# Four token-row chunks of an encoder's MLP moved from its start to its end, with VectorE block transposes in place of identity products

## The chip, the core and the metric

The kernel runs on one core of a Trainium2 chip. Its time is the device time of one execution in microseconds (us). A core has a matrix engine (TensorE, PE in the profile; its weight loads are listed apart as PEld), VectorE (DVE), ScalarE (ACT), GpSimd (POOL) and SyncE (SP), which here issues nearly all transfers. Matrix products write to PSUM; everything else lies in SBUF, with 128 partitions.

## The reference

Two layers of an encoder over 256 tokens of width 1024, each of a token mixer (pooling, dilated attention, gates) and a gated MLP, with RMSNorm ahead of each and a residual addition behind it. The change touches the MLP:

```python
def _conv_ffn(xn, w_up, conv_w, conv_b, w_down):
    a, gval = jnp.split(xn @ w_up, 2, axis=-1)
    a = lax.conv_general_dilated(a, conv_w[:, None, :], window_strides=(1,),
                                 padding=((CONV_WIDTH // 2, CONV_WIDTH // 2),),
                                 dimension_numbers=('NWC', 'WIO', 'NWC'),
                                 feature_group_count=D_FF) + conv_b
    return (jax.nn.gelu(a) * gval) @ w_down
```

`a` and `gval` are 256 x 2816 each. The convolution has width 3 and runs over the tokens, channel by channel.

## The kernel before, in words

**Layout.** Activations are kept with channels on the partitions, 128 at a time, and the tokens of even and odd number apart: `t` is 0 or 1, and token 2m + t stands at place m of half t. The 2816 MLP channels are NF = 22 chunks of 128. Each value is split into a high part in the matrix engine's fp32r type and the rest as a low part, and a product of two such values is taken as three products: high by high, high by low, low by high.

**Weights.** `Weights` (L81 on) streams all weights through the core in one order, which the calls of `W.use` write down (L235 to L282). A load brings 1 MB by one transfer on SyncE's queue (L117) into one of three raw buffers; it holds two pieces of 128 x 1024 elements. `open_next` turns a piece into its high part on ScalarE (L177) and its low part on VectorE (L178), in one of five buffers or, where a slot is named, in the buffer of a big tile that is idle then. `get` hands out the next piece and splits up to three more ahead (four more if they have a slot). A new load waits until the splits have read the raw buffer that it takes.

**A chunk by projection.** `proj` (L495 on, its products in `two_sums`, L487 to L493) takes one weight piece as the stationary operand and x2, the normed activations in high and low part, as the moving one: eight products of 512 columns (L491) and eight of 256 (L493). The result has channels on the partitions. `add_up` sums its two halves with one ScalarE copy (L513) and one VectorE addition (L514). The PSUM pool `mmp` has four buffers, and each projection takes one.

**The MLP's entry.** Of the first ENTRY = 4 chunks, `a` comes from another form: the products with x2 as the stationary operand and 512 columns of w_up as the moving one (`v_sum`, L583 on, L588; 24 products for each t). Their result has tokens on the partitions ("token rows"). For t = 0 this starts while the residual addition of the token mixer still runs (`begin_mlp`): x2's half t = 0 is complete earlier than t = 1. ScalarE copies the rows to SBUF (`keep_entry`, L1062), and `turn_entry` turns them to channels by four products with the identity matrix (L1068) and a VectorE copy from PSUM (L1070), once for each t. The group for t = 0 stands in the middle of the row products of t = 1; that for t = 1 stands behind the first projection, of chunk 0's `g`.

**The loop.** `up(f)` computes chunk f: it takes `a` (by projection from chunk 4 on), its `g` by projection, the convolution (L1094, L1095, L1098), the gelu in its tanh form (L1107 to L1112), the product with `g` (L1115), and the split of the result into high and low part (L1120, L1121). The loop takes two chunks at a time. From f = LAG = 6 on it adds two steps of `down` (`residual_mm`, L518 to L520), each with twelve products of 512 columns, for chunks f - 6 and f - 5. Behind the loop the last six steps follow; of the last four, the products are held back and taken output by output, so that the norm of the next sub-layer can begin early.

**Order.** PE, VectorE and ScalarE run their instructions in an order which a scheduler makes from the program's order and a cost model; a ready instruction can be drawn ahead of others. Each engine then runs its list in that order.

Of the kernel before, what the change touches and what calls it, by code (L numbers as in the profile page):

```python
# [10 lines left out]
F32 = mybir.dt.float32  # L11
# [5 lines left out]
P = 128  # L17
D = 1024
S = 256
# [8 lines left out]
NF = DFF // P  # L28
# [9 lines left out]
PAIRS = (2, 4, 0, 1, 3, 5)  # L38
LAG = 6
ENTRY = 4  # L40
HALVES = (slice(0, 512), slice(512, D))
SEGMENTS = (HALVES, (slice(0, 512), slice(512, 768), slice(768, D)))

# [161 lines left out]
def encoder(ctx, tc, x, w_in, w_pool, pool_scale, w_a, w_b, w_o, norm1, norm2, w_up, conv_w,  # L205
            conv_b, w_down, rel_bias, norm_f, onehot, edges, out):
    nc = tc.nc
    const = ctx.enter_context(tc.tile_pool(name="const", bufs=1))
    wpool = ctx.enter_context(tc.tile_pool(name="weights", bufs=1))
    big = ctx.enter_context(tc.tile_pool(name="big", bufs=1))  # L210
    sm = ctx.enter_context(tc.tile_pool(name="small", bufs=2))
    acc = ctx.enter_context(tc.tile_pool(name="acc", bufs=4, space=bass.MemoryType.PSUM))
    mmp = ctx.enter_context(tc.tile_pool(name="mmp", bufs=4, space=bass.MemoryType.PSUM))
# [3 lines left out]
    W = Weights(tc, wpool, big)  # L217

    def cols(w, c0):

        src = w[:, c0 : c0 + 256].rearrange("(k p) c -> p k c", p=P)
        return W.add(
            src, (8, 256), [((lambda t, j=j: t[:, :, j * P : (j + 1) * P]), (8, P)) for j in (0, 1)]
        )

    def rows(w, r0, n=2, c0=0, width=1024, tag=None, pieces=2):

        src = w[r0 : r0 + n * P, c0 : c0 + width].rearrange("(k p) c -> p k c", p=P)
        h = n // pieces
        return W.add(  # L230
            src, (n, width), [((lambda t, j=j: t[:, j * h : (j + 1) * h, :]), (h, width)) for j in range(pieces)],
            tag,
        )

    for l in range(DEPTH):  # L235
        for g in range(NG):
            c0 = C_V + g * 512
            slots = (("m2", 0, 2), ("m2", 1, 2), ("ybig",), ("at2",)) if g == 0 else ()
            for j in range(2):
                tag = "k1" if l == 0 and g == 1 and j == 0 else None  # L240
                W.use(rows(w_in[l], j * 512, 4, c0, 512, tag), slots[2 * j : 2 * j + 2])
        if l == 0:
            W.n_scaled = len(W.pieces)
        for c in range(3, -1, -1):
            W.use(cols(w_in[l], c * 256))
        for n, c in enumerate(PAIRS):
            pool = ([], [])
            if n == 1:
                pool = W.add(
                    w_pool[l].rearrange("g (k p) c -> p (g k) c", p=P), (8, 256),  # L250
                    [((lambda t, j=j: t[:, 4 * j : 4 * j + 4, :]), (4, 256)) for j in range(2)],
                )
                pool = (pool[:1], pool[1:])
            W.use(pool[0] + cols(w_in[l], C_Q + c * 256))
            W.use(pool[1] + cols(w_in[l], C_K + c * 256))
        for c in range(4):
            W.use(cols(w_a[l], c * 256))
        for c in range(4):
            W.use(cols(w_in[l], C_GP + c * 256))
        for c in range(2):  # L260
            W.use(cols(w_in[l], C_GA + c * 512))
            W.use(cols(w_in[l], C_GA + c * 512 + 256))
            src = w_b[l][:, c * 512 : (c + 1) * 512].rearrange("(k p) c -> p k c", p=P)
            W.use(
                W.add(
                    src, (4, 512),
                    [((lambda t, j=j: t[:, :, j * 256 : (j + 1) * 256]), (4, 256)) for j in (0, 1)],
                )
            )
        for c in range(4):  # L270
            W.use(rows(w_o[l], c * 256))
        slots = (("v1",), ("ybig",), ("at2",))
        for j in range(2):
            W.use(rows(w_up[l], j * 512, 4, 0, 512), slots[2 * j : 2 * j + 2])
        for f in range(0, NF, 2):
            a = cols(w_up[l], f * P) if f >= ENTRY else []
            g = cols(w_up[l], DFF + f * P)
            W.use([a[0], g[0], a[1], g[1]] if a else g)
            if f >= LAG:
                W.use(rows(w_down[l], (f - LAG) * P))  # L280
        for f in range(NF - LAG, NF, 2):
            W.use(rows(w_down[l], f * P))  # L282
# [10 lines left out]
    ident = const.tile([P, P], F32, name="ident")  # L293
# [201 lines left out]
    def proj(x2):  # L495

        i, (wh, wl) = W.get()
        ps = mmp.tile([P, 2, S], F32, tag="mm", name="proj_ps")
        two_sums(ps, lambda k: wh[:, k, :], lambda k: wl[:, k, :], x2, KD)
        W.free(i)  # L500
        return ps[:, 0], ps[:, 1]
# [78 lines left out]
    def v_tile():  # L580
        return acc.tile([P, 512], F32, tag="acc", name="v_ps")

    def v_sum(ps, x2, t, n, piece):  # L583

        _, (wh, wl) = piece
        passes = [(0, wh, 0), (0, wl, 0), (1, wh, 0), (0, wh, 1), (0, wl, 1), (1, wh, 1)]
        for m, (part, w, j) in enumerate(passes):
            nc.tensor.matmul(  # L588
                ps, x2[:, 2 * n + j, part, t, :], w[:, j, :], start=(n + m == 0),
                stop=(n == 3 and m == 5),  # L590
            )

    def two_parts(tag, name):

# [163 lines left out]
    for l in range(DEPTH):  # L758
# [21 lines left out]
        if l == 0:  # L780
            with tc.manual_schedule():
                begun = begin_values_of_x()
            x2 = first_values(*begun, keep_values)
        else:
            for g in range(NG):
                held = begun[0] if g == 0 else [W.get() for _ in range(4)]
                for t in range(2):
                    if g + t == 0:
                        ps = begun[1]
                    else:  # L790
                        ps = v_tile()
# [16 lines left out]
        for gi in range(3, -1, -1):  # L808
# [8 lines left out]
            cur, n = u, S + 2 * PAD  # L817
# [13 lines left out]
            if hw > 1:  # L831
                e = edge[:, gi, hw : w - 1].unsqueeze(1).to_broadcast([P, 2, hw - 1])
                r = slice(o + S - hw + 1, o + S)
# [109 lines left out]
        for pair in ((0, 1), (2, 3)):  # L943
            a, b = pair
# [110 lines left out]
        acts = {}  # L1055


        a_first = big.tile([P, ENTRY, S], F32, tag="gates", name="a_first")

        def keep_entry(ps):  # L1060
            r = sm.tile([P, ENTRY * P], F32, tag="p", bufs=3, name="a_rows")
            nc.scalar.copy(out=r, in_=ps)  # L1062
            return r

        def turn_entry(t, r):
            pt = mmp.tile([P, ENTRY, P], F32, tag="mm", name="a_turn")
            for f in range(ENTRY):
                nc.tensor.transpose(pt[:, f, :], r[:, f * P : (f + 1) * P], ident)  # L1068
            av = a_first.rearrange("p f (m t) -> p f m t", t=2)[:, :, :, t]
            nc.vector.tensor_copy(av, pt)  # L1070

        held, ps = entry
        first = keep_entry(ps)
        ps = v_tile()
        for n in range(4):
            v_sum(ps, x2, 1, n, held[n])
            if n == 1:
                turn_entry(0, first)
        for i, _ in held:
            W.free(i)  # L1080
        last = keep_entry(ps)
        g_first = [proj(x2)]
        turn_entry(1, last)

        def up(f):
            w0, w1, w2, b = (prm[:, l, j * NF + f : j * NF + f + 1] for j in range(4))
            if f < ENTRY:
                a = a_first[:, f, :]
            else:
                a = sm.tile([P, S], F32, tag="u", name="a")  # L1090
                add_up(in_order(a), [halves(b) for b in proj(x2)])
            sums = g_first.pop() if f == 0 else proj(x2)
            y = sm.tile([P, S], F32, tag="s", name="y")
            nc.scalar.activation(y, a, AF.Identity, bias=b, scale=w1)  # L1094
            nc.vector.scalar_tensor_tensor(  # L1095
                out=y[:, 1:], in0=a[:, : S - 1], scalar=w0, in1=y[:, 1:], op0=ALU.mult, op1=ALU.add
            )
            nc.vector.scalar_tensor_tensor(  # L1098
                out=y[:, : S - 1], in0=a[:, 1:], scalar=w2, in1=y[:, : S - 1],
                op0=ALU.mult, op1=ALU.add,  # L1100
            )
            g = sm.tile([P, 2, P], F32, tag="p", bufs=3, name="g")
            add_up(g, [halves(a) for a in sums])

            c = float(np.sqrt(2.0 / np.pi))
            y2 = sm.tile([P, S], F32, tag="us", name="y2")
            nc.scalar.activation(y2, y, AF.Square, scale=float(np.sqrt(0.044715)))  # L1107
            nc.vector.scalar_tensor_tensor(  # L1108
                out=y2, in0=y2, scalar=1.0, in1=y, op0=ALU.add, op1=ALU.mult
            )  # L1110
            nc.scalar.activation(y2, y2, AF.Tanh, scale=c)  # L1111
            nc.vector.scalar_tensor_tensor(  # L1112
                out=y2, in0=y2, scalar=1.0, in1=y, op0=ALU.add, op1=ALU.mult
            )
            nc.vector.scalar_tensor_tensor(  # L1115
                out=g, in0=in_order(y2), scalar=0.5, in1=g, op0=ALU.mult, op1=ALU.mult
            )
            n = f % NH
            ah, al = (x[n >= HPG][:, n - HPG * (n >= HPG)] for x in (acth, actl))
            nc.scalar.copy(out=ah, in_=g)  # L1120
            nc.vector.tensor_sub(out=al, in0=g, in1=ah.bitcast(F32))  # L1121
            acts[f] = (ah, al)
# [58 lines left out]
```

## Time and profile before

| | |
|---|---|
| median of three runs | 881.05 us (880.59 to 881.76) |
| the profiled execution | 880.87 us |
| its span, first to last instruction | 879.1 us |
| mean granted TensorE clock | 0.998 of full speed |
| bytes read from HBM | 162.74 MB |

The profile is of one execution. Rows with one line of the kernel, one engine and one operation are groups: busy time, mean ns of one, and what ended the idle time before them. The chain is the sequence of work that ended last, followed back from the last instruction. In the chain and the timeline the first column is the start in us from the span's start, the second the length in us. A view of waits lists the waiting engine and line, the releaser, us in total, number of times, and the longest one. In a view of stretches each engine's busy us stand with the number of its instructions, then the granted clock, the busy share of the transfer engines, and GB/s.

### The profile page before, as it was taken

To read this page: it belongs to the slowest core of one execution; us is meant where nothing else is said; L and a number is where in the kernel's file an instruction comes from. 1 tells how busy PE (TensorE), PEld (TensorE's weight loads), DVE (VectorE), ACT (ScalarE), POOL (GpSimd) and SP (SyncE) were. 2 spreads that over 40 slices of the span, in tenths; PEclk is the share of its full clock that TensorE was granted. 3 is DMA by queue.
4 is the path that set the end of the run, shared out by engine and by line. 5 is a ranking of instruction groups with operands and counts; after the bars stand their busy time and mean duration, and the time that the engine had idled before them with its cause. 6 is when DMAs were issued, how large, how long until landed. Compare 5 with 4: busy or idle time off the path is not lost.

```text
span 879.1 us, 12834 instructions
## 1 busy us (share of the span) xinstructions
PE 871.3 (99%) x4842; PEld 759.4 (86%) x4842; DVE 677.3 (77%) x1150; ACT 520.3 (59%) x913; POOL 14.7 (2%) x45
## 2 busy tenths in 40 slices
PE   9999999999999999999999999999999999999997
PEld 7888899988888888888888898999888888888886
DVE  6998786767869987787756977776678698878774
ACT  6755554556648766666545565554566486656653
POOL 2000000000000000000000000000000000000000
PEclk9999999999999999999999999999999999999999
DMA  9669744355554665565736565443556447466541
GB/s 325 237 232 304 229 145 157 131 190 183 172 198 149 212 215 192 168 215 192 240 120 227 157 200 184 154 158 124 191 189 199 164 147 255 170 195 204 178 144 48
DMA packets 126090, 164.64 MB, mean 187 GB/s; under 512 B 3254, under 2 KB 106374, under 8 KB 125900
## 3 DMA queue, kind: packets, MB, share of 16 engines
q1 hardware_dynamic: 126012, 163.82, 56.2%
q8 instruction: 38, 0.62, 0.3%
q14 instruction: 24, 0.20, 0.1%
q10 hardware_dynamic: 16, 0.00, 0.0%
HBM read 162.74 MB, written 3.69 MB: 189 GB/s over the span
## 4 chain that ended last, share of the span: by engine, by line
PE 96%; DVE 2%; DMA 1%; ACT 0%; issue 0%; POOLq 0%; POOL 0%; DVEq 0%; ACTq 0%; SPq 0%
PE proj_ps L491 38%; PE proj_ps L493 20%; PE res_ps L519 6%; PE v_ps L588 6%; PE res_ps L518 6%; PE res_ps L520 6%; PE v_ps L750 2%; PE b_ps L491 2%; PE v_ps L663 1%; DMA raw<-in_w_in_dram 1%; PE b_ps L493 1%; PE o_ps L934 1%; PE s_ps L884 1%; PE pt_ps L913 1%; PE s_ps L879 1%; PE o_ps L930 1%
## 5 line engine op out<-in xcount | busy, mean ns | idle before, releaser
L178 DVE TENSOR_TENSOR wl<-raw,wh 128x1024 fp32r<-128x1024 f32 x274 | 334.5, 1224 | 139.6 <-ACT wh L177 136.4
L177 ACT CAST wh<-raw 128x1024 fp32r<-128x1024 f32 x274 | 286.2, 1049 | 197.0 <-PE proj_ps L491 134.3
L491 PE MATMUL proj_ps<-x,wh 128*128 128x512 f32 x1408 | 353.4, 393 | 0.0
L491 PEld LDWEIGHTS proj_ps<-x,wh 128*128 128x128 f32 x1408 | 254.1, 189 | 46.2
L493 PEld LDWEIGHTS proj_ps<-x,wl 128*128 128x128 f32 x1408 | 192.1, 190 | 13.9
L493 PE MATMUL proj_ps<-x,wl 128*128 128x256 f32 x1408 | 196.5, 282 | 0.0
L518 PE MATMUL res_ps<-wh,actq 128*128 128x512 f32 (+1 forms) x184 | 70.2, 381 | 0.0
L519 PE MATMUL res_ps<-wl,actq 128*128 128x512 f32 (+1 forms) x184 | 70.1, 381 | 0.0
L520 PE MATMUL res_ps<-wh,actk 128*128 128x512 f32 (+1 forms) x184 | 69.9, 380 | 0.0
L520 PEld LDWEIGHTS res_ps<-wh,actk 128*128 128x128 f32 x184 | 34.6, 188 | 6.6
L518 PEld LDWEIGHTS res_ps<-wh,actq 128*128 128x128 f32 x184 | 34.7, 188 | 6.2
L519 PEld LDWEIGHTS res_ps<-wl,actq 128*128 128x128 f32 x184 | 34.7, 188 | 6.0
L491 PE MATMUL proj_ps<-po,wh 128*128 128x512 f32 x128 | 33.1, 401 | 0.0
L1111 ACT ACTIVATE y<-y 128x256 f32<-128x256 f32 x44 | 18.3, 416 | 24.5 <-DVE y L1108 24.5
L1094 ACT ACTIVATE y<-a,prm 128x256 f32<-128x256 f32 x36 | 21.6, 599 | 16.1 <-DVE a L514 16.1
L425 ACT ACTIVATE junk<-h 128x512 f32<-128x512 f32 (+1 forms) x20 | 10.9, 547 | 27.7 <-DVE h L423 27.7
L518 PE MATMUL res_ps<-wh,m 128*128 128x512 f32 (+1 forms) x72 | 26.5, 368 | 0.0
L491 PEld LDWEIGHTS proj_ps<-po,wh 128*128 128x128 f32 x128 | 22.9, 189 | 4.2
L519 PE MATMUL res_ps<-wl,m 128*128 128x512 f32 (+1 forms) x72 | 26.3, 366 | 0.0
L520 PE MATMUL res_ps<-wh,m 128*128 128x512 f32 (+1 forms) x72 | 26.3, 365 | 0.0
L588 PE MATMUL v_ps<-wh,x 128*128 128x512 f32 x80 | 25.7, 392 | 0.0
L1095 DVE SCALAR_TENSOR_TENSOR y<-a,prm,y 128x255 f32<-128x255 f32 x36 | 17.3, 480 | 8.0 <-ACT y L1094 8.0
(208 smaller groups left out, 1106.7 us busy)
## 6 DMA issues: line engine op xcount, KB each, us to landing
raw<-in_w_in_dram SPq DMA_DIRECT2D x58, 1024.0 KB, 5.6
raw<-in_w_up_dram SPq DMA_DIRECT2D x44, 1024.0 KB, 5.0
raw<-in_w_down_dram SPq DMA_DIRECT2D x22, 1024.0 KB, 4.9
raw<-in_w_a_dram SPq DMA_DIRECT2D x8, 1024.0 KB, 5.0
raw<-in_w_o_dram SPq DMA_DIRECT2D x8, 1024.0 KB, 4.9
raw<-in_w_b_dram SPq DMA_DIRECT2D x4, 1024.0 KB
sk<-fd SPq DMA_DIRECT2D x1, 2560.0 KB
raw<-in_w_pool_dram SPq DMA_DIRECT2D x2, 1024.0 KB
```

The lines of the kernel that those rows point to most:

```text
L177: lambda: nc.scalar.copy(out=h, in_=src),
L178: lambda: nc.vector.tensor_sub(out=l, in0=src, in1=h.bitcast(F32)),
L491: nc.tensor.matmul(ps, wh(k), x2[:, k], start=(k == 0), stop=False)
L493: nc.tensor.matmul(ps[:, 1], wl(k), x2[:, k, 0], start=False, stop=(k == nk - 1))
L518: nc.tensor.matmul(ps, ah, wh, start=first, stop=False)
L519: nc.tensor.matmul(ps, ah, wl, start=False, stop=False)
L520: nc.tensor.matmul(ps, al, wh, start=False, stop=last)
L588: nc.tensor.matmul(ps, x2[:, 2 * n + j, part, t, :], w[:, j, :], start=(n + m == 0), stop=(n == 3 and m == 5),)
L750: nc.tensor.matmul(ps[t], a[:, k, t, :], w[:, j, :], start=(k + m == 0), stop=(k == KD - 1 and m == 2),)
L1094: nc.scalar.activation(y, a, AF.Identity, bias=b, scale=w1)
L1095: nc.vector.scalar_tensor_tensor(out=y[:, 1:], in0=a[:, : S - 1], scalar=w0, in1=y[:, 1:], op0=ALU.mult, op1=ALU.add)
L1111: nc.scalar.activation(y2, y2, AF.Tanh, scale=c)
```

## The change

The token-row form is used for the last four chunks (18 to 21, FIRST = NF - ENTRY = 18) instead of the first four. The row products stay at the MLP's entry, in the same place and number; they now read columns 18 x 128 to 22 x 128 of w_up. The loop takes `a` by projection for chunks 0 to 17, so the weight order has pairs of `a` and `g` from chunk 0 on, and `g` alone for chunks 18 to 21.

ScalarE copies the rows of both halves into one tile, `a_rows`, in the big buffer `m2` (before: two small tiles in buffers `p`). The identity products and the copies behind them are gone, and all row products of t = 1 now follow each other, with chunk 0's `a` as the first projection behind them. VectorE turns the rows by a transpose instruction that works on blocks of 32 x 32: `blocks` makes sixteen of them, one for each pair of 32 token places and 32 channels, each on 32 partitions x 256 elements (two t, four chunks, 32 places). One is issued in each of `up(0)` to `up(15)`, behind the addition for `a`.

```diff
+FIRST = NF - ENTRY
...
-            W.use(rows(w_up[l], j * 512, 4, 0, 512), slots[2 * j : 2 * j + 2])
+            W.use(rows(w_up[l], j * 512, 4, FIRST * P, 512), slots[2 * j : 2 * j + 2])
         for f in range(0, NF, 2):
-            a = cols(w_up[l], f * P) if f >= ENTRY else []
+            a = cols(w_up[l], f * P) if f < FIRST else []
...
+    def blocks(out, in_):
+
+        for i in range(4):
+            for j in range(4):
+                a, b = slice(32 * i, 32 * i + 32), slice(32 * j, 32 * j + 32)
+                nc.vector.transpose(out=out[b, :, :, a], in_=in_[a, :, :, b])
+                yield
...
-        a_first = big.tile([P, ENTRY, S], F32, tag="gates", name="a_first")
-
-        def keep_entry(ps):
-            r = sm.tile([P, ENTRY * P], F32, tag="p", bufs=3, name="a_rows")
-            nc.scalar.copy(out=r, in_=ps)
-            return r
-
-        def turn_entry(t, r):
-            pt = mmp.tile([P, ENTRY, P], F32, tag="mm", name="a_turn")
-            for f in range(ENTRY):
-                nc.tensor.transpose(pt[:, f, :], r[:, f * P : (f + 1) * P], ident)
-            av = a_first.rearrange("p f (m t) -> p f m t", t=2)[:, :, :, t]
-            nc.vector.tensor_copy(av, pt)
+        a_last = big.tile([P, ENTRY, S], F32, tag="gates", name="a_last")
+        a_rows = big.tile([P, 2, ENTRY, P], F32, tag="m2", name="a_rows")
 
         held, ps = entry
-        first = keep_entry(ps)
-        ps = v_tile()
-        for n in range(4):
-            v_sum(ps, x2, 1, n, held[n])
-            if n == 1:
-                turn_entry(0, first)
+        for t in range(2):
+            if t:
+                ps = v_tile()
+                for n in range(4):
+                    v_sum(ps, x2, t, n, held[n])
+            nc.scalar.copy(out=a_rows[:, t], in_=ps)
         for i, _ in held:
             W.free(i)
-        last = keep_entry(ps)
-        g_first = [proj(x2)]
-        turn_entry(1, last)
+        turning = blocks(a_last.rearrange("p f (m t) -> p t f m", t=2), a_rows)
 
         def up(f):
             w0, w1, w2, b = (prm[:, l, j * NF + f : j * NF + f + 1] for j in range(4))
-            if f < ENTRY:
-                a = a_first[:, f, :]
+            if f >= FIRST:
+                a = a_last[:, f - FIRST, :]
             else:
                 a = sm.tile([P, S], F32, tag="u", name="a")
                 add_up(in_order(a), [halves(b) for b in proj(x2)])
-            sums = g_first.pop() if f == 0 else proj(x2)
+                next(turning, None)
+            sums = proj(x2)
```

## The prediction

> **What bounds the kernel now.** I read the page's head and its chain first, then TensorE's (PE's) own list of waits.
>
> ```profile
> span 879.1 us, 12834 instructions
> PE 871.3 (99%) x4842; PEld 759.4 (86%) x4842; DVE 677.3 (77%) x1150; ACT 520.3 (59%) x913; POOL 14.7 (2%) x45
> ...
> PE 96%; DVE 2%; DMA 1%; ACT 0%; issue 0%; POOLq 0%; POOL 0%; DVEq 0%; ACTq 0%; SPq 0%
> ```
>
> ```profile
> PE gain_ps L333 <- DVE ones L319: 1.0, 1, 1.0
> PE v_ps L663 <- ACT xuh L619: 0.2, 1, 0.2
> ```
>
> PE is busy for 99% of the span, carries 96% of the chain, and waited for others for 1.2 us in all, at the very start. In both MLPs it waits for nobody. So a product taken off PE shortens the kernel by the room it takes in PE's stream, and work added to VectorE (DVE) is free until it makes PE wait. Next, the removed operations by tile (minimum/median/maximum ns), and the stretch of the chain (start, length, both us) in which they stand in layer 0, then in layer 1.
>
> ```profile
> L1068 PEld LDWEIGHTS a_turn<-ident,a_rows x16: 137/140/143, 265.4 to 703.4; 128*128 128x128 f32 x16
> L1068 PE MATMUL a_turn<-ident,a_rows x16: 270/272/273, 265.6 to 703.5; 128*128 128x128 f32 x16
> L1070 DVE COPY a_first<-a_turn x4: 681/682/685, 266.9 to 704.1; 128x512 f32<-128x512 f32 x4
> ```
>
> ```profile
> 262.99 2.75 PE v_ps L588 x12
> 265.75 0.44 PE a_turn L1068 x4
> 266.18 2.77 PE v_ps L588 x12
> 268.95 1.81 PE proj_ps L491 x8
> 270.77 0.96 PE proj_ps L493 x8
> 271.72 0.44 PE a_turn L1068 x4
> 272.16 1.85 PE proj_ps L491 x8
> 274.02 0.95 PE proj_ps L493 x8
> 274.97 1.84 PE proj_ps L491 x8
> ```
>
> ```profile
> 694.60 2.75 PE v_ps L588 x12
> ...
> 700.56 1.81 PE proj_ps L491 x8
> ...
> 706.57 1.84 PE proj_ps L491 x8
> ```
>
> One identity product has a record of 272 ns, but four hold the chain for only 0.44 us: the record overlaps its neighbours, and 0.11 us is what one really takes from PE.
>
> **The change part by part.** *Removed from PE:* 16 identity products in four groups. The floor is 4 x 0.44 = 1.76 us. A better figure comes from the same sequence without groups, which the trace holds where layer 1 begins:
>
> ```profile
> 448.37 27.23 PE v_ps L588 x120
> 475.60 1.81 PE proj_ps L491 x8
> ...
> 481.16 0.93 PE proj_ps L491 x4
> ```
>
> There 24 row products take 24 x 27.23 / 120 = 5.45 us, and the first two projections take 481.16 - 475.60 = 5.56: 11.01 us together. The same work with the two groups takes 274.97 - 262.99 = 11.98 in layer 0 and 706.57 - 694.60 = 11.97 in layer 1. So 0.97 + 0.96 = **1.93 us** leave PE. I take this value and keep 1.76 as the other end; the 0.17 between them is the slower restart behind each group. The diff takes out the only call of the identity products here, so that they stay on is excluded.
>
> [...]
>
> *Moved on PE:* the chunks of the row products now stand last. Each layer still runs 24 + 24 row products, 18 + 22 projections and 22 down steps, and as many switches between projections and down steps, so the order itself costs PE nothing. The loads are as many and as large.
>
> *Added to DVE:* 16 block transposes a layer, each 32 partitions x 256 elements; removed are two copies of 0.68 us. The trace shows no such instruction. The nearest rows, and DVE's load in two stretches, the entry and the steady part of layer 0's MLP (length, then PE, PEld, DVE, ACT busy in turn):
>
> ```profile
> L1121 DVE TENSOR_TENSOR actk<-g,actq 128x256 fp32r<-128x256 f32 x44 | 18.3, 419 | 0.7 <-ACT actq L1120 0.7
> L178 DVE TENSOR_TENSOR wl<-raw,wh 128x1024 fp32r<-128x1024 f32 x274 | 334.5, 1224 | 139.6 <-ACT wh L177 136.4
> ```
>
> ```profile
> 268.95:302.60 33.65, 33.65 (x196) 29.64 (x195) 32.22 (x63) 26.46 (x51) 0.00 (x0) 1.00 0.64 215
> 352.40:369.00 16.60, 16.60 (x90) 14.32 (x90) 13.22 (x22) 10.38 (x19) 0.00 (x0) 1.00 0.57 191
> ```
>
> A block T costs 0.42 us if it streams its 256 elements like any other operation (the value I take), 0.68 if it passes them twice (the 512-element copy), 1.22 at four times. Less than 0.42 changes nothing, as DVE isn't the bound.
>
> The cover. DVE is busy 32.22 of 33.65 us in the entry, so the room there is small. In the steady stretch two chunks need 13.22 us of DVE in 16.60: six weight splits (7.34) and 5.88 of element work, 2.94 a chunk. Chunks 0 to 5 will now need 12 x 1.224 + 6 x 2.94 = 32.3 plus 6T on DVE, against 12 projections x 2.78 (half of the 5.56 above) = 33.4 on PE. At T = 0.42 DVE falls behind by 1.4 us, at 0.68 by 3.0, at 1.22 by 6.2. Before, these six chunks had eight projections (22.2 us) with eight splits and four `a` additions less: 9.8 + 6 x 2.94 - 4 x 0.42 = 25.8, behind by 3.6, and PE didn't wait. What stock is there?
>
> ```profile
> 286.21 1.22 DVE L178 TENSOR_TENSOR wl<-raw,wh 128x1024 fp32r<-128x1024 f32 x1
> ```
>
> ```profile
> 291.73 1.84 PE proj_ps L491 x8
> ```
>
> This split serves the projection at 291.73, whose second half starts at 293.57: done at 287.43, 6.1 us early, the shortest lead that I found there. So blocks spread over the chunks cost nothing up to T of 1.2 us. From chunk 6 on 13.22 + 2T stands against 16.60. In chunks 18 to 21 PE has two projections less per pair, 16.60 - 5.56 = 11.0 us, DVE four splits and at most the 5.88, 10.8, and their `a` is ready long before. Hidden: **0**.
>
> *Buffers and queues.* The rows now lie in the buffer of m2. The last products that read it precede the row products whose copy fills it; its next writer in the first layer is a split of the next layer's weights, long after chunk 15:
>
> ```profile
> 424.54 1.22 DVE L178 TENSOR_TENSOR m<-raw,m 128x1024 fp32r<-128x1024 f32 x1
> ```
>
> With chunk 0 as a pair of weights, the first two loads are used alternately, so SyncE's fourth load waits for the third split instead of the second:
>
> ```profile
> 264.64 2.36 DVE L178 TENSOR_TENSOR wl<-raw,wh 128x1024 fp32r<-128x1024 f32 x2 [0.25 <-ACT wh L177]
> ...
> 267.52 2.35 DVE L178 TENSOR_TENSOR wl<-raw,wh 128x1024 fp32r<-128x1024 f32 x2
> ```
>
> ```profile
> raw<-in_w_up_dram SPq DMA_DIRECT2D x44, 1024.0 KB, 5.0
> ```
>
> The third split ends near 268.7; 5 us later, at 273.7, the load is there. It serves the sixth projection, near 282.3 (268.44 + 5 x 2.78, where 268.44 = 262.99 + 5.45), whose cast (1.05 us) may start as late as 281.3: 7.6 us of cover. Only the loads of later chunks queue behind it on SyncE. Its steady price is seen in the pairs of later chunks: none. What is late next on PE: x2's second half for the row products, which now start their second dozen 0.44 earlier, at 265.75.
>
> ```profile
> 263.70 0.69 DVE L463 TENSOR_TENSOR x<-xt_ps,x 128x512 fp32r<-128x512 f32 x1 [1.19 <-ACT x L462]
> ```
>
> It is done at 264.39, 1.36 us early.
>
> **Sum:** -1.93 us. The profiled execution took 880.87 us (879.1 of span and 1.8 around it), so it would take 878.94; the median of the runs, 881.05, is 0.18 above it: **879.1 us**, 0.22% faster. A measurement tells about 0.2% from no change, 1.76 us, so the border is at 879.29 and the forecast lies barely beyond it. With scatter of the runs (880.59 to 881.76) its own range is 878.4 to 880.0.
>
> **The rivals.**
>
> *Identity products at full price (faster).* Were each worth its 272 ns, 4.35 us would go: 876.7. Against it stands the spacing of 0.11 us. Chance 0.03.
>
> *The cover comes back (same).* If two of the four groups filled a pause that PE would otherwise have made (x2's second half, or the second projection's split), only half is gained: 881.05 - 0.97 = 880.1. The 1.36 us above speaks against it. Chance 0.08.
>
> *Blocks in a bunch (slower).* DVE's order isn't the program's: a memset that the program has in the next layer's pooling runs in chunks 18 to 21.
>
> ```profile
> 418.75 0.07 DVE L811 MEMSET u<- 128x16 f32 x1
> ```
>
> All sixteen blocks are ready once the second copy of rows is done. Before, it ended 0.63 us behind the last row product (268.95):
>
> ```profile
> 268.99 0.59 ACT L1062 COPY a_rows<-v_ps 128x512 f32<-128x512 f32 x1 [1.54 <-PE v_ps L588]
> ```
>
> Now it will end near 268.44 + 0.63 = 269.1. If they are issued together there, DVE is shut for 16T. PE's fifth projection, at 268.44 + 4 x 2.78 = 279.56, needs the PSUM buffer of the first, which one DVE addition (0.42) must have read. So PE waits from 16T > 279.56 - 0.42 - 269.1 = 10.0 on, that is T > 0.63, and the gain of 0.97 a layer is eaten at T > 0.69. At 0.68 it costs 0.9 us a layer (880.9), at 1.22 it costs 9.5 a layer: 881.05 - 1.93 + 19.0 = 898.1. Both conditions are needed; DVE's short idle times before 272 would draw a few blocks forward, hardly all. Chance 0.08, 0.06 of it slower.
>
> [...]
>
> *Late loads (slower).* The alternating pairs leave one raw buffer ahead. Were landings of the entry's loads above 5.0 + 7.6 = 12.6 us, each us more would cost one a layer; at 15 us 879.1 + 2 x 2.4 = 883.9. The steady stretch, 57% of the transfer engines at 191 GB/s, speaks against it. Chance 0.03.
>
> **How the numbers follow.** The forecast has 0.78. About 0.55 of it falls below 879.29, 0.23 above (end 1.76, scatter). Faster: 0.55 + 0.03 = 0.58. Same: 0.23 + 0.08 + 0.02 = 0.33. Slower: 0.06 + 0.03 = 0.09. The range takes in the given-back cover and the bunch at 0.68, and the scatter below: 878.3 to 880.9. Outside it are the full-price case and most of both slower ones.
>
> **What would show it.** Right: PE's own waits in the MLPs stay at nothing; from the first of the second 24 row products to the third projection some 11.0 us instead of 11.98; sixteen blocks a layer of about 0.42 us, spread over 269 to 400 us; the chunks 18 to 21 at 11.0 us a pair. Wrong: PE waits for `add_up` or a split between 270 and 300 us, blocks above 0.63 us in one bunch, casts that wait for a load of w_up.

## The result and the profile after

The changed kernel takes **879.07 us** (median of 20 runs, 878.22 to 880.62), the kernel before 880.96 (median of 20 runs, one of which took 4965.7 us). The ratio is 0.998, 95% interval 0.9973 to 0.9987: faster by 0.2%, 1.89 us between the medians, with 879.1 forecast. The profiled execution took 878.79 us with a span of 877.0.

The head of the page and its chain by engine:

```profile
span 877.0 us, 12827 instructions
PE 868.5 (99%) x4826; PEld 756.8 (86%) x4826; DVE 688.2 (78%) x1178; ACT 520.0 (59%) x913; POOL 15.5 (2%) x45
...
PE 95%; DVE 2%; DMA 1%; ACT 1%; issue 0%; POOLq 0%; POOL 0%; DVEq 0%; ACTq 0%; SPq 0%
```

PE has 16 products less and is still busy for 99% of the span. VectorE has 28 instructions more (32 blocks for 4 copies) and 10.9 us more work, and the span is 2.1 us shorter. The waits of PE (line, releaser, us, times, longest):

```profile
PE gain_ps L334 <- DVE ones L320: 1.0, 1, 1.0
PE pool_ps L485 <- DVE pll L852: 0.6, 1, 0.6
PE v_ps L672 <- ACT xuh L628: 0.2, 1, 0.2
PE v_ps L672 <- ACT m L186: 0.2, 1, 0.2
```

All lie in the first 78 us, at the start of the program and in the token mixer of layer 0, none in an MLP. The list of PE's weight loads (PEld), which also shows waits that this list leaves out, has none in an MLP either. One group of ScalarE's waits is new, for loads of w_up:

```profile
ACT wh L178 <- DMA raw<-in_w_up_dram: 1.6, 3, 0.9
```

These are casts of weights in the loops of both MLPs; none of the three waits reached PE. The chain at the MLP's entry, in layer 0 and then in layer 1:

```profile
262.71 5.47 PE v_ps L589 x24
268.18 1.81 PE proj_ps L492 x8
269.99 0.95 PE proj_ps L494 x8
270.95 1.84 PE proj_ps L492 x8
272.79 0.95 PE proj_ps L494 x8
273.74 1.84 PE proj_ps L492 x8
```

```profile
693.47 5.47 PE v_ps L589 x24
...
704.50 1.84 PE proj_ps L492 x8
```

The 24 row products follow each other without a break. From the first of them to the third projection it is 273.74 - 262.71 = 11.03 us, and 704.50 - 693.47 = 11.03, where it was 11.98 and 11.97: 0.95 + 0.94 = **1.89 us**. The blocks by tile, and where VectorE ran the first of layer 0, between the splits and element operations:

```profile
L599 DVE STREAM_TRANSPOSE a_last<-a_rows x32: 425/437/442, 268.9 to 739.6; 32x256 f32<-32x256 f32 x32
```

```profile
264.36 4.63 DVE L179 TENSOR_TENSOR wl<-raw,wh 128x1024 fp32r<-128x1024 f32 x4 [0.25 <-ACT wh L178]
268.91 1.32 DVE L599 STREAM_TRANSPOSE a_last<-a_rows 32x256 f32<-32x256 f32 x3
270.25 1.23 DVE L179 TENSOR_TENSOR wl<-raw,wh 128x1024 fp32r<-128x1024 f32 x1
271.49 0.89 DVE L599 STREAM_TRANSPOSE a_last<-a_rows 32x256 f32<-32x256 f32 x2
...
272.87 1.34 DVE L599 STREAM_TRANSPOSE a_last<-a_rows 32x256 f32<-32x256 f32 x3
...
274.75 0.43 DVE L599 STREAM_TRANSPOSE a_last<-a_rows 32x256 f32<-32x256 f32 x1
```

A block takes 0.44 us. Nine of the sixteen run within the first 6.3 us behind the rows' copy, ahead of their chunks, and the last ends at 309.3: the scheduler drew them forward into VectorE's free time, as the rival with the bunch had feared for all of them.

### The profile page after: what moved, and what is told of

Same layout as the page of the kernel before. It is cut to its first block, busy times and chain, and to the rows that moved or that the text cites. A ratio compares the mean times of both kernels' runs of the same rounds, so it can differ in the third digit from the quotient of the medians.

```text
span 877.0 us, 12827 instructions
## 1 busy us (share of the span) xinstructions
PE 868.5 (99%) x4826; PEld 756.8 (86%) x4826; DVE 688.2 (78%) x1178; ACT 520.0 (59%) x913; POOL 15.5 (2%) x45
## 4 chain that ended last, share of the span: by engine, by line
PE 95%; DVE 2%; DMA 1%; ACT 1%; issue 0%; POOLq 0%; POOL 0%; DVEq 0%; ACTq 0%; SPq 0%
PE proj_ps L492 38%; PE proj_ps L494 20%; PE res_ps L519 6%; PE res_ps L520 6%; PE v_ps L589 6%; PE res_ps L521 6%; PE v_ps L759 2%; PE b_ps L492 2%; PE v_ps L672 1%; DMA raw<-in_w_in_dram 1%; PE b_ps L494 1%; PE o_ps L943 1%; PE s_ps L893 1%; PE pt_ps L922 1%; PE s_ps L888 1%; PE o_ps L939 1%
## 5 line engine op out<-in xcount | busy, mean ns | idle before, releaser
L426 ACT ACTIVATE junk<-h 128x512 f32<-128x512 f32 (+1 forms) x20 | 10.9, 546 | 26.9 <-DVE h L424 26.8
L1117 ACT CAST actq<-g 128x256 fp32r<-128x256 f32 x44 | 17.6, 401 | 10.7 <-DVE g L1112 10.6
```

## The experiments

The theory: the gain is the room of the identity products in PE's stream, and blocks are free until VectorE is shut or behind for longer than the buffers cover. Each run's time stands beside the kernel before, run on the same chip. Where a run is compared with the changed kernel, that is the 879.07 us above; the kernel before differs by 0.1 us at most between these sets of runs. The code cuts show the difference from the changed kernel, but for the fourth experiment, which starts from the kernel before.

**The place alone.** The last four chunks, but with `keep_entry`, `turn_entry` and the first group's call as in the kernel before, so with the identity products and copies in their two old places:

```diff
-        turning = blocks(a_last.rearrange("p f (m t) -> p t f m", t=2), a_rows)
+        last = keep_entry(ps)
+        p_first = [proj(x2)]
+        turn_entry(1, last)
...
-                add_up(in_order(a), [halves(b) for b in proj(x2)])
-                next(turning, None)
+                ps = p_first.pop() if f == 0 else proj(x2)
+                add_up(in_order(a), [halves(b) for b in ps])
```

> The row chunks are the last four, but they are still turned by identity products and VectorE copies in the two old places. Theory (the gain is the room of the identity products on PE, the place costs and gains nothing): as before, 881.0 us, ratio 0.999 to 1.001, with 11.98 us from the second dozen-pair of row products to the third projection. Rival (the gain comes from the place: the entry is no longer fed by four g projections alone, so VectorE falls behind less): 879.1 us, as the changed kernel.

881.34 us beside 880.90; ratio 1.0003 (0.9994 to 1.0012). The chain in layer 0:

```profile
262.40 2.75 PE v_ps L589 x12
265.15 0.44 PE a_turn L1077 x4
265.59 2.77 PE v_ps L589 x12
...
274.37 1.84 PE proj_ps L492 x8
```

274.37 - 262.40 = 11.97 us, as before. Moving the chunks is worth nothing by itself.

**The blocks alone.** The first four chunks, all blocks at the entry:

```diff
-        turning = blocks(a_last.rearrange("p f (m t) -> p t f m", t=2), a_rows)
+        run(blocks(a_first.rearrange("p f (m t) -> p t f m", t=2), a_rows))
...
+            if f < ENTRY:
+                a = a_first[:, f, :]
```

> The row chunks stay the first four, but VectorE turns them, all sixteen blocks a layer at the entry. Theory: PE gets back its 0.97 us a layer and the bunch of 16 x 0.44 = 7.0 us fits under the 10.0 us after which PE's fifth projection would wait; VectorE is then behind by 3.6 - 1.4 + 7.0 = 9.2 us in chunks 0 to 5, just under 6.1 + 3.6 = 9.7: 879.1 us, at worst 880.0. Rival (the block form pays only where nothing waits for the turned chunks): PE waits in the entry for additions or splits, 2 us a layer or more, 883 us or above.

879.64 us beside 880.90; ratio 0.9985 (0.9976 to 0.9994). The time lies between the theory's 879.1 and its worst case of 880.0, and the rival's 883 falls. VectorE's row in layer 0, PE's rows at the first down step of layer 1, and the waits of the weight loads for a split:

```profile
269.17 7.19 DVE L598 STREAM_TRANSPOSE a_first<-a_rows 32x256 f32<-32x256 f32 x16
...
279.78 0.75 DVE L1103 SCALAR_TENSOR_TENSOR y<-y,y 128x256 f32<-128x256 f32 x2
```

```profile
732.80 0.39 PE L518 MATMUL res_ps<-wh,actq 128*128 128x512 f32 x1
733.25 0.50 PE L519 MATMUL res_ps<-wl,actq 128*128 128x512 f32 x1
733.58 0.39 PE L520 MATMUL res_ps<-wh,actk 128*128 128x512 f32 x1
```

```profile
PEld res_ps L519 <- DVE wl L178: 0.7, 2, 0.4
```

The second product starts 0.45 us after the first instead of 0.23: it waited some 0.2 us for the split of its weights, and so once in each layer. VectorE was behind by 9.2 us by the theory's count, and that just used up the cover (9.7 by the same count). The form gives the gain in either place; in the first four chunks it leaves no stock. Its median is 0.6 us above the changed kernel's. The two intervals overlap, but the traces bear part of it out: from layer 0's row products to those that open layer 1 it is 447.77 - 262.97 = 184.80 us here and 447.24 - 262.71 = 184.53 in the changed kernel.

**No turning at all.** Chunks 18 to 21 read the unturned rows, so part of the computation is left out:

```diff
-            nc.scalar.copy(out=a_rows[:, t], in_=ps)
+            nc.scalar.copy(out=a_rows[:, :, t], in_=ps.rearrange("p (f m) -> p f m", f=ENTRY))
...
-        turning = blocks(a_last.rearrange("p f (m t) -> p t f m", t=2), a_rows)
...
-                a = a_last[:, f - FIRST, :]
+                a = a_rows[:, f - FIRST].rearrange("p t m -> p (t m)")
...
-                next(turning, None)
```

> Leaves the turning out altogether: chunks 18 to 21 take the unturned rows as if they were channels. Theory (the blocks are hidden): as the changed kernel, 879.1 us, ratio to before 0.9975 to 0.9985. Rival (the blocks cost part of what the identity products gave back): 0.5 to 2 us below the changed kernel, 877 to 878.5.

879.31 us beside 880.90; ratio 0.9984 (0.9975 to 0.9993). Not below the changed kernel: the 14 us of blocks cost nothing that shows. The traces say it more closely: the stretch above takes 447.17 - 262.71 = 184.46 us without blocks and 184.53 with them, and from layer 1's entry to the end of the span it is 876.9 - 693.40 = 183.50 against 877.0 - 693.47 = 183.53.

**The price of an identity product.** The kernel before, each done four times:

```diff
-            for f in range(ENTRY):
+            for f in 4 * tuple(range(ENTRY)):
```

> The kernel before, with every identity product done four times into the same place: 48 more in the whole run, in the same four groups. Theory (0.11 us of PE each): 12 x 0.44 = 5.3 us more, 886.3. Rival (each costs its record of 0.272 us): 13.1 us more, 894.1.

886.15 us beside 880.90, 5.25 us more; ratio 1.0059 (1.0043 to 1.0074). Two of the four groups in the chain:

```profile
266.04 1.75 PE a_turn L1068 x16
...
273.28 1.75 PE a_turn L1068 x16
```

1.75 / 16 = 0.109 us each, while their records still say 0.273. The rival with the full price falls.

**The bunch.** All blocks issued ahead of chunk 0: once; then twice (`range(2)` in the added line); then once and the first eight again.

```diff
-        turning = blocks(a_last.rearrange("p f (m t) -> p t f m", t=2), a_rows)
+        for _ in range(1):
+            run(blocks(a_last.rearrange("p f (m t) -> p t f m", t=2), a_rows))
...
-                next(turning, None)
```

> The changed kernel with all sixteen blocks of a layer issued together at the entry, ahead of chunk 0. Theory (DVE may be shut for 10.0 us before PE's fifth projection lacks its buffer, and may fall behind by some 9.7 us in chunks 0 to 5): 16 x 0.45 = 7.2 us of blocks, behind by 32.3 + 7.2 - 33.4 = 6.1: no wait of PE, 879.1 us. Rival (the spread over sixteen chunks is what hides the blocks): slower than the changed kernel by 2 us or more.

879.52 us beside 881.00; ratio 0.9982 (0.9973 to 0.9991). No wait of PE or of its weight loads in an MLP: spreading the blocks isn't what hides sixteen of them.

> The same bunch with every block done twice: 32 blocks, 14.3 us a layer. Theory: 14.3 - 10.0 = 4.3 us of wait a layer by the buffer, or 32.3 + 14.3 - 33.4 = 13.2 of arrears against 9.7, 3.5 a layer: 879.1 + 7 to 8.6 = 886 to 888 us. Rival (there is no such limit near 10 us, a bunch is hidden whatever its size): 879.1.

893.31 us beside 881.00; ratio 1.0139 (1.0125 to 1.0153). A limit is there, but the cost, 14.2 us above the changed kernel, is more than the 7 to 8.6 expected. VectorE's row in layer 0, then PE's in both layers, then two stretches of layer 0 (length; PE, PEld, DVE, ACT, POOL busy; granted clock):

```profile
269.81 14.95 DVE L599 STREAM_TRANSPOSE a_last<-a_rows 32x256 f32<-32x256 f32 x32
284.79 0.43 DVE L515 TENSOR_TENSOR a<-proj_ps,a 128x256 f32<-128x256 f32 x1
```

```profile
268.92 1.98 PE L492 MATMUL proj_ps<-x,wh 128*128 128x512 f32 x8
...
285.27 3.78 PE L492 MATMUL proj_ps<-x,wh 128*128 128x512 f32 x8 [5.04 <-DVE a L515]
288.85 1.63 PE L494 MATMUL proj_ps<-x,wl 128*128 128x256 f32 x8
290.31 2.00 PE L492 MATMUL proj_ps<-x,wh 128*128 128x512 f32 x8
...
723.38 3.68 PE L492 MATMUL proj_ps<-x,wh 128*128 128x512 f32 x8 [5.04 <-DVE a L515]
726.88 1.13 PE L494 MATMUL proj_ps<-x,wl 128*128 128x256 f32 x8
727.85 2.00 PE L492 MATMUL proj_ps<-x,wh 128*128 128x512 f32 x8
```

```profile
280.10:285.20 5.10, 0.12 (x2) 0.00 (x0) 4.79 (x12) 0.53 (x2) 0.00 (x0) 0.80 0.00 0
285.30:290.40 5.10, 5.10 (x17) 4.33 (x18) 5.10 (x8) 0.97 (x2) 0.00 (x0) 0.54 0.00 0
```

PE ran four projections and waited with the fifth until the addition had read the first one's PSUM buffer, as the prediction's rival with the bunch said: 5.04 us in each layer. So the rival without a limit falls. The rest is new. Behind the pause of layer 0 the granted clock is 0.54, and the fifth projection lasts from 285.27 to 290.31, 5.04 us instead of 2.78: 2.3 us more. In layer 1 the fifth projection lasts 727.85 - 723.38 = 4.47 us: 1.7 more. 10.1 + 2.3 + 1.7 = 14.1 us, and 14.2 were measured.

```diff
+        run(blocks(a_last.rearrange("p f (m t) -> p t f m", t=2), a_rows))
+        again = blocks(a_last.rearrange("p f (m t) -> p t f m", t=2), a_rows)
+        for _ in range(8):
+            next(again)
```

> The bunch at the entry with 24 blocks a layer (the first eight done twice). Theory (the buffer of the first projection sets the limit near 10 us; the slow products behind the pause of 5 us in the bunch of 32 came from the pause): 24 x 0.467 = 11.2 us of blocks and 0.5 of addition against 10.3 to the fifth projection: 1.4 us of wait a layer, and after so short a pause no slow products: 879.1 + 2.8 = 881.9. Rival (the slow products come with any pause, or with a long row of blocks): their 2.4 us a layer on top, 886.7. Second rival (the limit isn't the buffer; the cost rises in proportion from 16 to 32 blocks): half of 14.2, 886.2.

881.91 us beside 880.99; ratio 1.001 (1.000 to 1.002). PE's waits, and in layer 0 the first projection, the fifth behind the pause, and the sixth:

```profile
PE proj_ps L492 <- DVE a L515: 2.3, 2, 1.2
...
PE res_ps L520 <- DVE wl L179: 0.6, 1, 0.6
```

```profile
268.25 1.98 PE L492 MATMUL proj_ps<-x,wh 128*128 128x512 f32 x8
...
280.72 2.14 PE L492 MATMUL proj_ps<-x,wh 128*128 128x512 f32 x8 [1.17 <-DVE a L515]
...
283.63 2.00 PE L492 MATMUL proj_ps<-x,wh 128*128 128x512 f32 x8
```

From the first projection to the sixth it is 283.63 - 268.25 = 15.38 us, against 282.12 - 268.18 = 13.94 in the changed kernel: the wait for the buffer costs 1.44 a layer, 2.9 in all, and 2.84 lie between the medians. The profiled execution, 0.8 us above its median, also waits once for a split, 0.6 us in layer 0. The projection behind this short pause takes 283.63 - 280.72 = 2.91 us, nearly the usual 2.78. Both rivals, slow products after any pause and a cost in proportion, fall.

**Three times the blocks, spread.**

```diff
-                nc.vector.transpose(out=out[b, :, :, a], in_=in_[a, :, :, b])
+                for _ in range(3):
+                    nc.vector.transpose(out=out[b, :, :, a], in_=in_[a, :, :, b])
```

> The changed kernel with every block done three times where it stands, one chunk each: 48 blocks, 21.4 us a layer. Theory (what counts is arrears, not the sum): 18 x 0.45 = 8.1 us in chunks 0 to 5, behind by 7.0, under 9.7, and 13.22 + 2.7 = 15.9 against 16.60 after that: 879.1 us, if the blocks stay near their chunks; if they are all drawn forward, up to (20 - 9.7) x 2 = 21 us more, 900. Rival (every VectorE us in the MLP costs): 879.1 + 2 x 14.3 = 907.7.

880.09 us beside 881.00; ratio 0.9991 (0.9982 to 1.0001): 1.0 us above the changed kernel where 0 was expected and the rival said 28.6. From the row products of layer 0's entry to those that open layer 1, and from layer 1's entry to the end of the span:

```profile
263.91 5.47 PE v_ps L589 x24
...
449.09 27.23 PE v_ps L589 x120
...
695.32 5.47 PE v_ps L589 x24
```

449.09 - 263.91 = 185.18 against 447.24 - 262.71 = 184.53 in the changed kernel, and 879.1 - 695.32 = 183.78 against 877.0 - 693.47 = 183.53. Together that is 0.9 us more, with 28 us of additional VectorE work. Some 0.2 us in each layer arise at a down step, where a weight load waits for its split behind blocks; in layer 0:

```profile
360.91 1.86 DVE L600 STREAM_TRANSPOSE a_last<-a_rows 32x256 f32<-32x256 f32 x4
362.80 1.23 DVE L179 TENSOR_TENSOR wl<-raw,wh 128x1024 fp32r<-128x1024 f32 x1
...
364.08 0.19 PEld L520 LDWEIGHTS res_ps<-wl,actq 128*128 128x128 f32 x1 [0.28 <-DVE wl L179]
```

Another 0.4 lie where layer 1 opens, behind the last block: eighteen row products take 4.62 us there, 4.21 in the changed kernel and 4.10 to 4.35 in the other traces. Whether the blocks have a part in that isn't shown. The blocks are hidden almost wholly, but not free.

**The same exchange elsewhere.** On top of the change, attention's head 0 is turned by blocks:

```diff
+                if hh == 0:
+                    if t == 0:
+                        both.append(big.tile([P, 2, 2, 512], F32, tag="ybig", name="both"))
+                    p = both[0][:, 0, t]
...
+            if hh == 0:
+                pf = both[0][:, 1].rearrange("p t (k m) -> p (t k) m", k=4).rearrange("p (k t) m -> p k t m", t=2)
+                run(blocks(pf.rearrange("p k t m -> p t k m"), both[0][:, 0].rearrange("p t (k m) -> p t k m", k=4)))
+                nc.scalar.copy(out=pth, in_=pf[:, 0:2])
+                nc.vector.tensor_sub(out=ptl, in0=pf[:, 0:2], in1=pth.bitcast(F32))
+                ptiles[hh] = pth, ptl, pf[:, 2:4]
+                return
```

> The changed kernel, and attention's head 0 turned by VectorE blocks as well, from and to an idle big buffer, in place of its eight identity products a layer. Theory (an identity group is worth 0.44 to 0.49 us of PE, blocks are free where VectorE has room): 4 groups, 1.8 to 1.95 us more, 877.2 us. Rival (here somebody waits for the turned values: softmax, 7.2 us of blocks, cast and subtraction, 13 us at least, against the 11 to 17 us that PE's queue has before the head's weighing): PE waits for the low part, 1 to 10 us a layer, 880 to 899.

**877.60 us** beside 881.00; ratio 0.996 (0.9948 to 0.9973), the fastest version here: 1.5 us below the changed kernel's median. The start of a run scatters by about as much: the 24 row products of layer 0's MLP begin at 262.40 in one trace above and at 263.91 in another, behind the same work. So a stretch measures better, here from layer 1's first row products to its MLP entry:

```profile
447.46 27.23 PE v_ps L589 x120
...
692.80 5.47 PE v_ps L589 x24
```

692.80 - 447.46 = 245.34 us against 693.47 - 447.24 = 246.23: 0.89 for two groups, 0.45 each, as the theory's 0.44. PE has no wait in the attention, so the rival falls for this head. Heads 1 to 3 weren't tried: the author found no idle big buffer with room for them.

## Why the prediction was right

- **PE is the bound, and it is the spacing in the chain that counts.** 1.93 us were forecast from the same sequence without groups where layer 1 begins; 1.89 left the two entries and 1.89 lie between the medians. That the medians give the very same number is luck: the interval of the ratio allows 1.1 to 2.4 us. The identity products done four times gave 0.109 us each against the 0.11 taken.
- **The move costs nothing.** Shown by the place alone (1.0003).
- **Blocks are hidden.** 0.44 us each against the 0.42 chosen, no wait of PE in an MLP, and without them the kernel is no faster. They did not stay spread over 269 to 400 us: those of layer 0 began at 268.9, nine by 275.2, and the last ended at 309.3. So the cover that was counted chunk by chunk wasn't put to the test as forecast; that sixteen are hidden even in one bunch is why it didn't matter. Chunks 18 to 21 take 11.0 us a pair, as forecast (412.41 - 401.38 = 11.03 in layer 0).
- **The bunch rival** was right in mechanism and place: a limit near 10 us by the first projection's buffer, shown by 16, 24 and 32 blocks. Its price lacked a term, the slow products behind the pause of 5.0 us, 2.3 and 1.7 us in the two layers at 32 blocks. It didn't decide because sixteen blocks take 7.2 us.
- **The cover comes back.** PE's stretch is shorter by the whole 0.95, so it did not.
- **Late loads.** A sign named for being wrong did appear: casts waited for loads of w_up, 1.6 us in three waits, where the kernel before has none. They don't come from the weight order alone: the place alone, with the new order, has 4.4 us of them, but the blocks alone, with the old one, 7.1. In none of the three did PE wait for a load in an MLP, so the cover sufficed.

The forecast lay barely beyond the border of 0.2%, and so does the result, 1.89 us against 1.76; the interval reaches to both sides of it.

## What to carry to other kernels

Price an operation on the bounding engine by the difference between two stretches of the chain that hold the same work with and without it, not by its record: here 0.12 us (1.89 / 16) against 0.27. Work that is moved to an engine with free time was free here until a buffer that it held up was needed again, but for waits of 0.2 us for late weight splits; count that time (four PSUM buffers, 10 us here) and test it with two or three times the work. For effects of a fraction of a per cent, compare the same stretch between two marks in two traces: the scatter at the start, 1.5 us between the traces here, drops out.

## What the runs showed of the hardware that was not expected

- **Behind a pause of 5.0 us the products were slow.** In layer 0 the granted clock was 0.54 over the next 5.1 us and a projection took 5.04 us instead of 2.78, in layer 1 4.47; after 1.2 us of pause it took 2.91. In the MLPs no run has a pause between these two lengths.
- **Blocks did not overlap one another.** With the first four chunks 16 blocks took 7.19 us, 0.449 each and no less than the record of 0.437, while two element operations of 0.42 us take 0.75 together (the row with x2 above); the 32 of the bunch took 14.95 us, 0.467 each. In the changed kernel the first block begins at 268.91, before the split ahead of it ends (264.36 + 4.63 = 268.99), the fourth at 271.49, behind the end of its split (270.25 + 1.23 = 271.48). What decides whether a block starts early isn't shown.
